# Earlier load requests, and six low parts made by an adding DMA, in an encoder layer

## The chip, the cores and the metric

The kernel runs on one core of a Trainium2 chip. The core has a TensorE for matrix products, a VectorE, a ScalarE and a GpSimd for elementwise work, and a SyncE, which here only issues DMAs. The metric is the device time of one execution in microseconds (us), as the median of several runs. On a page of the profile the engines are PE (matmul), PEld (TensorE's weight loads), DVE (VectorE), ACT (ScalarE), POOL (GpSimd) and SP (SyncE). A q behind such a name is the part of the engine that issues DMAs.

## The reference

One layer over 512 tokens of width 1024, all in fp32. The important lines, with the attention cut:

```python
x = layer_norm(DN_ALPHA * x + 0.5 * swiglu(x, ffn1_wg[i], ffn1_wu[i], ffn1_wd[i]), ln1_g[i], ln1_b[i])
h = x @ w_in[i]
q, k, v, qi, ki, wi, bg, cg, u = jnp.split(h, split_points, axis=-1)
attn = dsa_attention(q, k, v, qi, ki, wi * IDX_SCALE)
conv = short_conv_mixer(bg, cg, u, conv_w[i])
mix = jnp.concatenate([attn, conv], axis=-1) @ w_out[i]
x = layer_norm(DN_ALPHA * x + mix, ln2_g[i], ln2_b[i])
x = layer_norm(DN_ALPHA * x + 0.5 * swiglu(x, ffn2_wg[i], ffn2_wu[i], ffn2_wd[i]), ln3_g[i], ln3_b[i])
x = x + jax.nn.sigmoid(x @ ple_gate_w[i]) * (p[i] @ ple_proj_w[i])
```

with `swiglu(x, wg, wu, wd) = (silu(x @ wg) * (x @ wu)) @ wd` and a hidden width of 2816 (22 chunks of 128).

## The kernel before

**Products.** Every fp32 matrix is held as two tiles of TensorE's faster type fp32r: `hi`, the matrix rounded, and `lo`, what the rounding left. `mm` (L127 to L133) makes each product as three passes, hi·hi, hi·lo and lo·hi. So each weight that comes from memory has to be split before TensorE can read it: `split` (L110 to L112) makes `hi` by a cast on ScalarE and then `lo = src - hi` by a subtraction on VectorE, which therefore waits for the cast.

**Units and pages.** `unit` (L114 to L122) takes a page, loads 512 KB of a weight into it by a DMA that SP issues (L118), takes two more pages for `hi` and `lo`, splits, and gives the first page back. Pages are 38 tiles of one size, handed out and given back first in, first out while the program is built, so a load waits until whoever read its page last is done.

**Order of work.** A scheduler lists all instructions by priority, which is by default the order in which the code is written. `tc.high_priority(offset=n)` moves what is written under it n places earlier. Each engine then works through its own list in order, and so do SP and POOL with the DMAs that they issue. A load and its split stand under the same offset: `AHEAD` and its sisters.

**Stages.** The time falls into the first FFN (to about 320 us) with its norm, the projection by `w_in`, the indexer and the attention, the out-projection with the second norm, the second FFN (from about 629 to 920 us) with its norm, and the gated embedding at the end. In an FFN the first two column chunks are made by `plain` (L256), with one unit of wg and one of wu each; the second FFN alone lets `plain` load the units of its chunk 0 itself, since for the first FFN they are made ahead and handed in. The other 20 chunks go in pairs through `two` (L309), which saves products by sums of weight blocks: for each of wg and wu the generator `weights` (L276) first loads two pages, then splits them and makes and splits the sums S1 to S4, in four steps, and `two` interleaves the steps of wg and wu. So the loads of wu stand behind wg's first step. The rows of wd are units as well (`wd_rows`, L359).

**The second norm's place.** The attention goes head by head: scores, softmax (VectorE L693, ScalarE's exponential L694, VectorE's scale L696), transposes (L710, with casts and subtractions behind them) and the product with the values (L722). Copies of an embedding stage that fills TensorE's gaps (L433) lie in between. Behind it come the four units of w_out, under `AHEAD_O2`, and for each of four token blocks the out-projection (two halves), a sum with x on VectorE and its statistics (L757, L758), the norm `ln_tb` (L156 to L162), and `Quarters.block` (L191), which transposes the block for the second FFN and splits and copies it (L204, L205, L224). In `ln_tb` VectorE adds up the statistics (L158, L159), POOL takes one over the square root by a power (L160), and VectorE scales and shifts the block (L161, L162). POOL does little else here.

Of the kernel before, what the change touches and what calls it, by code (L numbers as in the profile page):

```python
# [10 lines left out]
ALU = mybir.AluOpType  # L11
# [19 lines left out]
WSTEPS = (1, 2, 1)  # L31
BANKS = ((0, 1), (4, 5), (6,), (7, 2, 3))
AHEAD = 25
AHEAD_N = 150
AHEAD2 = 400
AHEAD_D1 = 125
# [9 lines left out]
AHEAD_C = 50  # L46
AHEAD_Q = 50
AHEAD_O = 0
AHEAD_O2 = 75
OB = ("fill", "all", "all", "all")  # L50
AHEAD_G = 200
NWARM = 2
# [11 lines left out]
def layer_kernel(ctx: ExitStack, tc: tile.TileContext, x, ln1_g, ln1_b, ffn1_wg, ffn1_wu, ffn1_wd, w_in,  # L64
# [21 lines left out]
    def page(shape, dt=F32R):  # L86
        i = free_pages.pop(0)
        t = sb.tile(shape, dt, tag=f"pg{i}", name=f"pg{i}_{count('pg')}")
        owner[id(t)] = (i, t)
        return t  # L90
# [19 lines left out]
    def split(hi, lo, src):  # L110
        nc.scalar.copy(hi, src)  # L111
        nc.vector.tensor_sub(lo, src, hi.bitcast(F32))  # L112

    def unit(src, shape, ahead=AHEAD):  # L114

        with tc.high_priority(offset=ahead):
            r = page(shape, F32)
            nc.sync.dma_start(r, src)  # L118
            hi, lo = page(shape), page(shape)
            split(hi, lo, r)  # L120
            free(r)
        return hi, lo  # L122

    def rows(w, r0, n):
        return w[r0:r0 + n * P].rearrange("(c p) n -> p c n", p=P)
# [118 lines left out]
    def ffn(X, wg, wu, wd, ln_g, ln_b, first, load_nat, groups, nplain, ahead, ahead_f, ahead_d):  # L244
# [11 lines left out]
        def plain(fc, ws, cuts, ah):  # L256

            for nm, w in mats:
                if nm not in ws:
                    ws[nm] = unit(rows(w[:, fc * P:(fc + 1) * P], 0, NDC), [P, NDC, P], ah)  # L260
            ps = {nm: bank("all") for nm, _ in mats}
            for n in range(2):
                for k in range(2):
# [12 lines left out]
        def weights(w, fc, ops, pages):  # L276

            r = []
            for c in (0, 4):
                r.append(page([P, 4, 2 * P], F32))  # L280
                nc.sync.dma_start(r[-1], rows(w[:, fc * P:(fc + 2) * P], c * P, 4))
            A11, A21, A12, A22 = (r[k][:, :, m * P:(m + 1) * P] for k in range(2) for m in range(2))
            a11 = page([P, 2, 4, P])
            split(a11[:, 0], a11[:, 1], A11)
# [24 lines left out]
        def two(fc, ah):  # L309

            W, pages = {nm: {} for nm, _ in mats}, []
            steps = [weights(w, fc, W[nm], pages) for nm, w in mats]
            with tc.high_priority(offset=ah):
                for n in WSTEPS:
                    for g in steps:
                        for _ in range(n):
                            next(g)
# [427 lines left out]


    g_t, b_t = bcast(ln2_g[0]), bcast(ln2_b[0])
    wo = [unit(rows(w_out, c * P, 1), [P, 1, 1024], AHEAD_O2) for c in range(4)]
    X = Quarters()
    for t in range(NTB):  # L750
        stats = ring("st", 4, [P, 2, 6])
# [63 lines left out]
```

## Time and profile before

| | |
|---|---|
| median of 3 runs | 1027.09 us (1025.58 to 1027.44) |
| profiled execution, its own time | 1025.29 us |
| its span | 1023.4 us |
| TensorE busy | 1004.4 us, 98% of the span |
| VectorE busy | 823.5 us, 80% |
| ScalarE busy | 442.6 us, 43% |
| GpSimd busy | 27.0 us, 3% |
| read from the chip's memory | 101.49 MB, 101 GB/s over the span |

The span runs from the first to the last record of the execution. The time of the execution has 1.9 us more, before and behind. Busy shares are means over stages that have different limits, so they say which engine is filled, not what an engine waits for at one place. For that there are the chain of waits (the chain of work that ended last, followed back from the last instruction), the table of stretches (busy time of each engine in a part of the span), and the rows of one engine in order of time, each with the idle time ahead of it and what ended that time. TensorE's granted clock is at its full 2.4 GHz throughout.

### The profile page before, as it was taken

Reading aid. Unit: us, or ns where it says so; the run is one execution under the profiler, and the core shown is the slowest. Engines: PE = TensorE matmul, PEld = TensorE weight load, DVE = VectorE, ACT = ScalarE, POOL = GpSimd, SP = SyncE. Lnnn points to the kernel's source line nnn. Section 1 sums busy time; section 2 is a strip of 40 time slices with the busy share of each in tenths; the row PEclk is TensorE's granted clock in tenths of the full one; section 3 lists DMA queues with packets and bytes.
Section 4 is the critical chain, followed back from the end, with each engine's and each line's share of the span. In section 5 each row is a group of like instructions: output and inputs, shape, how many; then the busy total and the mean of one; then the engine's idle time right before and its main releaser. Section 6 shows DMA issues by size and latency. Waiting matters only on the chain.

```text
span 1023.4 us, 15531 instructions
## 1 busy us (share of the span) xinstructions
PE 1004.4 (98%) x6311; PEld 902.3 (88%) x6311; DVE 823.5 (80%) x1289; ACT 442.6 (43%) x627; POOL 27.0 (3%) x35
## 2 busy tenths in 40 slices
PE   9999999999999989999999999999999999999998
PEld 7989999898998868888878788989999898998787
DVE  7997868978698946999679988896868969698952
ACT  7544334433355225432576736443425324246221
POOL 1000000000002100000000011000000000000100
PEclk9999999999999999999999999999999999999999
DMA  9532324323226322423112222431324322236111
GB/s 306 162 109 83 104 83 145 101 80 113 79 100 200 83 61 62 120 67 84 61 42 103 83 71 94 128 120 45 120 84 144 103 79 89 82 124 226 56 38 51
DMA packets 99606, 104.57 MB, mean 102 GB/s; under 512 B 5968, under 2 KB 82000, under 8 KB 99536
## 3 DMA queue, kind: packets, MB, share of 16 engines
q1 hardware_dynamic: 99536, 103.60, 32.0%
q8 instruction: 49, 0.80, 0.3%
q14 instruction: 21, 0.17, 0.1%
HBM read 101.49 MB, written 2.10 MB: 101 GB/s over the span
## 4 chain that ended last, share of the span: by engine, by line
PE 87%; DVE 4%; DMA 4%; ACT 3%; issue 1%; SPq 1%; POOL 0%; POOLq 0%; ACTq 0%; DVEq 0%
PE bk L132 84%; DVE pg L112 2%; ACT pg L111 2%; DMA pg<-in_ffn_wd_dram 1%; PE bk L524 1%; DMA pg<-in_ffn_wu_dram 1%; PE bk L525 1%; PE bk L722 1%; PE bk L146 1%; DMA pg<-in_x_t_dram 1%; DMA pg<-in_ple_proj_w_dram 1%; ACT a L694 0%; SPq L214 0%; DMA pg<-in_ple_gate_w_dram 0%; DVE nat L162 0%
## 5 line engine op out<-in xcount | busy, mean ns | idle before, releaser
L132 PE MATMUL bk<-pg,pg 128*128 128x256 f32 (+1 forms) x2832 | 496.7, 333 | 4.9 <-DVE pg L112 2.1
L132 PEld LDWEIGHTS bk<-pg,pg 128*128 128x128 f32 x2832 | 427.3, 190 | 57.2 <-DVE pg L112 3.9
L111 ACT CAST pg<-pg 128x1024 fp32r<-128x1024 f32 (+1 forms) x270 | 260.0, 976 | 303.3 <-PE bk L132 76.0
L112 DVE TENSOR_TENSOR pg<-pg,pg 128x1024 fp32r<-128x1024 f32 (+1 forms) x270 | 301.1, 1126 | 38.3 <-ACT pg L111 33.0
L132 PE MATMUL bk<-xq,pg 128*128 128x256 f32 x2208 | 274.7, 284 | 2.2 <-DVE mv L158 1.4
L132 PEld LDWEIGHTS bk<-xq,pg 128*128 128x128 f32 x2208 | 269.4, 192 | 5.9 <-ACT pg L433 1.8
L132 PE MATMUL bk<-xT,pg 128*128 128x512 f32 (+2 forms) x600 | 133.0, 381 | 0.2 <-ACT xT L111 0.2
L132 PEld LDWEIGHTS bk<-xT,pg 128*128 128x128 f32 (+1 forms) x600 | 110.1, 186 | 21.2 <-ACT xT L111 0.5
L132 PE MATMUL bk<-pg,xT 128*128 128x512 f32 (+1 forms) x312 | 69.8, 374 | 2.0 <-DVE nat L394 1.7
L132 PEld LDWEIGHTS bk<-pg,xT 128*128 128x128 f32 x312 | 54.9, 188 | 12.2 <-ACT pg L111 2.1
L336 ACT ACTIVATE a<-pg 128x512 f32<-128x512 f32 x40 | 25.2, 630 | 78.0 <-DVE pg L345 70.8
L111 ACT CAST pg<-hf 128x512 fp32r<-128x512 f32 (+1 forms) x56 | 34.6, 618 | 37.6 <-DVE hf L337 19.3
L112 DVE TENSOR_TENSOR pg<-hf,pg 128x512 fp32r<-128x512 f32 (+1 forms) x56 | 38.7, 690 | 4.1 <-ACT pg L111 3.8
L408 DVE SCALAR_TENSOR_TENSOR nat<-bk,nat 128x512 f32<-128x512 f32 x64 | 40.3, 682 | 1.2 <-PE bk L132 1.2
L345 DVE TENSOR_TENSOR pg<-bk,pg 128x512 f32<-128x512 f32 x20 | 13.8, 691 | 29.3 <-PE bk L132 29.0
L337 DVE TENSOR_TENSOR hf<-a,pg 128x512 f32<-128x512 f32 x40 | 27.5, 688 | 11.8 <-ACT a L336 11.7
L160 POOL TENSOR_TENSOR mv<-mv,mhalf 128x1 f32<-128x1 f32 x12 | 17.8, 1479 | 630.4 <-DVE mv L159 630.4
L112 DVE TENSOR_TENSOR pg<-bk,pg 128x512 fp32r<-128x512 f32 (+2 forms) x37 | 22.5, 626 | 12.8 <-ACT pg L111 12.4
L293 DVE TENSOR_TENSOR pg<-pg,pg 128x512 f32<-128x512 f32 x40 | 27.3, 686 | 5.6 <-DMA pg<-in_ffn_wg_dram 5.0
L299 DVE TENSOR_TENSOR pg<-pg 128x512 f32<-128x512 f32 x40 | 27.4, 685 | 2.5 <-PE bk L132 2.5
L294 DVE TENSOR_TENSOR pg<-pg,pg 128x512 f32<-128x512 f32 x40 | 27.4, 684 | 0.0
L300 DVE TENSOR_TENSOR pg<-pg,pg 128x512 f32<-128x512 f32 x40 | 27.0, 685 | 0.1
(100 smaller groups left out, 614.5 us busy)
## 6 DMA issues: line engine op xcount, KB each, us to landing
pg<-in_ffn_wd_dram SPq DMA_DIRECT2D x44, 512.0 KB, 4.0
pg<-in_ffn_wu_dram SPq DMA_DIRECT2D x43, 512.0 KB, 4.8
pg<-in_ffn_wg_dram SPq DMA_DIRECT2D x43, 512.0 KB, 3.9
pg<-in_w_in_dram SPq DMA_DIRECT2D x28, 512.0 KB, 3.6
pg<-in_w_out_dram SPq DMA_DIRECT2D x8, 512.0 KB, 3.9
pg<-in_ple_gate_w_dram SPq DMA_DIRECT2D x8, 512.0 KB, 3.7
pg<-in_x_t_dram SPq DMA_DIRECT2D x8, 256.0 KB, 5.8
nat<-in_x_dram SPq DMA_DIRECT2D x4, 512.0 KB, 9.2
```

The costliest lines, as they stand in the source:

```text
L111: nc.scalar.copy(hi, src)
L112: nc.vector.tensor_sub(lo, src, hi.bitcast(F32))
L132: nc.tensor.matmul(ps, lhsT=st[a], rhs=mv[b], start=first and i == 0 and k == 0, stop=last and i == n - 1 and k == 2)
L160: nc.gpsimd.tensor_tensor(mv[:, 3:4], mv[:, 2:3], mhalf, op=ALU.pow)
L293: nc.vector.tensor_add(S1, A21, A22)
L294: nc.vector.tensor_sub(S2, S1, A11)
L299: nc.vector.tensor_sub(S3, A11, A21)
L300: nc.vector.tensor_sub(S4, A12, S2)
L336: nc.scalar.activation(s_t, e[m][:, :, 0], AF.Silu)
L337: nc.vector.tensor_mul(h3, s_t, e[m][:, :, 1])
L345: nc.vector.tensor_add(e[0][:, 1], prod("S4", "B22"), u4)
L408: nc.vector.scalar_tensor_tensor(dst, acc[t], CY, dst, op0=ALU.mult, op1=ALU.add)
```

## The change

The change has three parts.

**Loads.** In `unit` the load stands under `ahead + LOAD` (60 places earlier) and the split under `ahead` as before. In `two` the loads of both weights are asked for first, under `ah + LOAD`, and the steps of splitting follow: `weights` now yields once behind its loads.

**Low parts.** `unit` can make `lo` in another way (`add`): ScalarE writes `lo = -r`, which rounds `-r`; a DMA that GpSimd issues then adds `r` to `lo` in place, and the sum of `r` and the rounded `-r` is what the rounding left. ScalarE also casts `r` to `hi`. VectorE has no part in it. Six units are made so: the four of w_out and, by `fc == 0`, those of wg and wu of the second FFN's chunk 0.

**The offset of w_out's units**, `AHEAD_O2`, goes from 75 to 150.

```diff
-AHEAD_O2 = 75
+AHEAD_O2 = 150
...
-    def unit(src, shape, ahead=AHEAD):
-
-        with tc.high_priority(offset=ahead):
+    def unit(src, shape, ahead=AHEAD, add=False):
+
+
+        with tc.high_priority(offset=ahead + LOAD):
             r = page(shape, F32)
             nc.sync.dma_start(r, src)
+        with tc.high_priority(offset=ahead):
             hi, lo = page(shape), page(shape)
-            split(hi, lo, r)
+            if add:
+                nc.scalar.mul(lo, r, -1.0)
+                nc.gpsimd.dma_start(lo, r, accum_op=ALU.add)
+                nc.scalar.copy(hi, r)
+            else:
+                split(hi, lo, r)
             free(r)
         return hi, lo
...
             for nm, w in mats:
                 if nm not in ws:
-                    ws[nm] = unit(rows(w[:, fc * P:(fc + 1) * P], 0, NDC), [P, NDC, P], ah)
+                    ws[nm] = unit(rows(w[:, fc * P:(fc + 1) * P], 0, NDC), [P, NDC, P], ah, fc == 0)
...
             for c in (0, 4):
                 r.append(page([P, 4, 2 * P], F32))
                 nc.sync.dma_start(r[-1], rows(w[:, fc * P:(fc + 2) * P], c * P, 4))
+            yield
...
             steps = [weights(w, fc, W[nm], pages) for nm, w in mats]
+            with tc.high_priority(offset=ah + LOAD):
+                for g in steps:
+                    next(g)
             with tc.high_priority(offset=ah):
                 for n in WSTEPS:
                     for g in steps:
...
-    wo = [unit(rows(w_out, c * P, 1), [P, 1, 1024], AHEAD_O2) for c in range(4)]
+    wo = [unit(rows(w_out, c * P, 1), [P, 1, 1024], AHEAD_O2, True) for c in range(4)]
```

What stands in a row on three engines around the second norm follows, before and after. The changed file is 13 lines longer, so the same code has other line numbers after: L113 is the cast of `split` (L111 before), L121 the load of a unit (L118), L169 the power (L160), L707 the exponential (L694), L446 the copy (L433); L125 to L127 are the new negation, adding DMA and cast. In the names, `pg_548`, `pg_551`, `pg_554` and `pg_557` are the loaded units of w_out, with `hi` and `lo` in the two numbers behind each; `pg_568` and `pg_571` are wg and wu of the second FFN's chunk 0, `pg_575` is wg of chunk 1; `a_5572` is the softmax tile of the last head but one, `a_5668` that of the last.

ScalarE at the end of the attention, before: the first cast of a w_out unit stands behind all casts of the last head but one.

```order
L694 ACTIVATE a_5572,ss_5573<-a_5572,ss_5573 128x384
L433 COPY pg_534_5614<-bk_5615 128x512
L694 ACTIVATE a_5572,ss_5573<-a_5572,ss_5573 128x512
L111 CAST pg_527_5565<-hf_5567 64x512
L111 CAST pg_535_5628<-bk_5623 128x512
L111 CAST pg_536_5636<-bk_5631 128x512
L111 CAST pg_537_5642<-bk_5639 128x256
L433 COPY pg_534_5614<-bk_5645 128x512
L111 CAST pg_549_5796<-pg_548_5794 128x1024
```

ScalarE at the same place, after.

```order
L707 ACTIVATE a_5572,ss_5573<-a_5572,ss_5573 128x384
L125 ACTIVATE pg_550_5797<-pg_548_5794 128x1024
L113 CAST pg_527_5565<-hf_5567 64x512
L127 CAST pg_549_5796<-pg_548_5794 128x1024
L707 ACTIVATE a_5572,ss_5573<-a_5572,ss_5573 128x512
L446 COPY pg_534_5614<-bk_5615 128x512
L113 CAST pg_535_5628<-bk_5623 128x512
L113 CAST pg_536_5636<-bk_5631 128x512
L113 CAST pg_537_5642<-bk_5639 128x256
```

The negation and the cast of that unit now stand ahead of the fourth exponential and of the three casts behind it.

POOL around the second norm, before: nothing stands between the power of the first norm and the four of the second.

```order
L160 TENSOR_TENSOR mv_3704<-mv_3704,mhalf 128x1
L160 TENSOR_TENSOR mv_5851<-mv_5851,mhalf 128x1
L160 TENSOR_TENSOR mv_5906<-mv_5906,mhalf 128x1
L160 TENSOR_TENSOR mv_5959<-mv_5959,mhalf 128x1
L160 TENSOR_TENSOR mv_6016<-mv_6016,mhalf 128x1
```

POOL at the same place, after.

```order
L169 TENSOR_TENSOR mv_3704<-mv_3704,mhalf 128x1
L126 DMA pg_550_5797<-pg_548_5794 128x1024
L126 DMA pg_553_5804<-pg_551_5801 128x1024
L126 DMA pg_556_5811<-pg_554_5808 128x1024
L126 DMA pg_559_5818<-pg_557_5815 128x1024
L126 DMA pg_570_6083<-pg_568_6080 128x1024
L126 DMA pg_573_6090<-pg_571_6087 128x1024
L169 TENSOR_TENSOR mv_5855<-mv_5855,mhalf 128x1
```

All six adding DMAs stand ahead of the second norm's first power.

SP from the second load of w_out's units to the first ones of the second FFN, with what each load waits for, before.

```order
L118 DMA pg_557_5812<-in_w_out_dram 128x1024 [waits DMAHW4_49,PE_49]
L153 DMA pg_546_5790<-in_ln_g_dram 128x1024 [waits DMAHW5_49,PE_49]
L118 DMA pg_548_5794<-in_w_out_dram 128x1024 [waits PE_49]
L118 DMA pg_554_5806<-in_w_out_dram 128x1024 [waits DVE_49,PE_49]
L118 DMA pg_575_6193<-in_ffn_wg_dram 128x8x128 [waits DMAHW4_49,DVE_49]
L118 DMA pg_568_6076<-in_ffn_wg_dram 128x8x128 [waits DMAHW1_49,PE_49]
```

SP at the same place, after.

```order
L121 DMA pg_557_5815<-in_w_out_dram 128x1024 [waits DMAHW4_49,PE_49]
L162 DMA pg_546_5790<-in_ln_g_dram 128x1024 [waits DMAHW5_49,PE_49]
L121 DMA pg_548_5794<-in_w_out_dram 128x1024 [waits PE_49]
L121 DMA pg_554_5808<-in_w_out_dram 128x1024 [waits DVE_49,PE_49]
L121 DMA pg_575_6199<-in_ffn_wg_dram 128x8x128 [waits DMAHW4_49,DMASW3_49,Activation_49]
L121 DMA pg_568_6080<-in_ffn_wg_dram 128x8x128 [waits DMAHW1_49,PE_49]
L121 DMA pg_571_6087<-in_ffn_wu_dram 128x8x128 [waits DMAHW2_49,PE_49]
```

The order of the loads is the same. The load of `pg_575`, whose page held a unit of w_out, waited for VectorE's subtraction of that unit; now it waits for the fourth adding DMA (DMASW3) and for ScalarE.

## Rows read from the trace of the kernel before

**Rows 1.** The page's first part: busy us (share of the span) xinstructions.

```profile
PE 1004.4 (98%) x6311; PEld 902.3 (88%) x6311; DVE 823.5 (80%) x1289; ACT 442.6 (43%) x627; POOL 27.0 (3%) x35
```

**Rows 2.** Stretches: length, busy PE, PEld, DVE, ACT, POOL, PEclk, DMA share, GB/s.

```profile
20.00:318.00 298.00, 298.00 (x2142) 282.77 (x2141) 245.60 (x327) 126.08 (x155) 0.91 (x2) 1.00 0.35 113
...
577.00:598.00 21.00, 19.93 (x104) 15.86 (x103) 17.88 (x38) 14.07 (x30) 0.00 (x0) 1.00 0.32 96
598.00:609.00 11.00, 10.49 (x48) 8.37 (x47) 10.36 (x18) 1.64 (x2) 1.46 (x1) 1.00 0.04 10
609.00:629.00 20.00, 17.57 (x113) 15.17 (x112) 17.85 (x25) 10.26 (x18) 4.37 (x3) 1.00 0.09 27
...
629.00:920.00 291.00, 291.00 (x2080) 275.69 (x2079) 237.33 (x314) 122.47 (x152) 0.00 (x0) 1.00 0.33 105
```

**Rows 3.** The chain of waits, 580 to 600 us: start us, us, what.

```profile
585.10 1.14 DVE pg L112
...
594.40 4.80 DMA pg<-in_ffn_wu_dram
```

**Rows 4.** SP's waits, 550 to 600; its rows; DMA issues with us to landing.

```profile
SPq L118 <- DVE pg L112: 17.3, 3, 9.7
...
572.12 8.66 SPq L118 DMA_DIRECT2D pg<-in_w_out_dram  x2
590.18 3.83 SPq L118 DMA_DIRECT2D pg<-in_ffn_wg_dram  x2
...
pg<-in_w_out_dram SPq DMA_DIRECT2D x1, 512.0 KB, 4.4
...
pg<-in_w_out_dram SPq DMA_DIRECT2D x1, 512.0 KB, 3.1
...
pg<-in_ple_proj_w_dram SPq DMA_DIRECT2D x1, 512.0 KB, 5.2
```

**Rows 5.** Groups by form, 577 to 629 us: xcount | busy, mean ns | idle before.

```profile
L112 DVE TENSOR_TENSOR pg<-pg,pg 128x1024 fp32r<-128x1024 f32 x8 | 9.7, 1220 | 1.2 <-ACT pg L111 1.2
L111 ACT CAST pg<-pg 128x1024 fp32r<-128x1024 f32 x6 | 6.3, 1054 | 2.7 <-DMA pg<-in_ffn_wu_dram 1.6 <-DMA pg<-in_ffn_wg_dram 1.1
```

**Rows 6.** VectorE in time: start us, us, what, xcount, [idle before <-releaser].

```profile
585.02 2.35 DVE L112 TENSOR_TENSOR pg<-pg,pg 128x1024 fp32r<-128x1024 f32 x2
...
597.75 0.69 DVE L757 SCALAR_TENSOR_TENSOR nat<-bk,nat 128x512 f32<-128x512 f32 x1 [0.62 <-PE bk L132]
...
600.30 1.23 DVE L112 TENSOR_TENSOR pg<-pg,pg 128x1024 fp32r<-128x1024 f32 x1 [0.46 <-ACT pg L111]
...
605.15 1.28 DVE L161 SCALAR_TENSOR_TENSOR nat<-nat,mv,pg 128x1024 f32<-128x1024 f32 x1
...
606.95 1.27 DVE L162 SCALAR_TENSOR_TENSOR nat<-nat,mv,pg 128x1024 f32<-128x1024 f32 x1
...
616.84 1.23 DVE L112 TENSOR_TENSOR pg<-pg,pg 128x1024 fp32r<-128x1024 f32 x1 [0.59 <-ACT pg L111]
...
629.27 0.69 DVE L205 TENSOR_TENSOR pg<-bk,pg 128x512 fp32r<-128x512 f32 x1 [1.68 <-ACT pg L204]
```

**Rows 7.** ScalarE in time.

```profile
575.90 0.73 ACT L694 ACTIVATE a<-a,ss 128x512 f32<-128x512 f32 x1
...
577.12 1.33 ACT L111 CAST pg<-bk 128x512 fp32r<-128x512 f32 x3
...
583.88 0.57 ACT L111 CAST pg<-bk 128x512 fp32r<-128x512 f32 x1
```

**Rows 8.** TensorE in time.

```profile
577.76 0.50 PE L722 MATMUL bk<-pg,pg 128*128 128x512 f32 x1 [0.19 <-ACT pg L111]
...
586.29 2.35 PE L132 MATMUL bk<-pg,pg 128*128 128x512 f32 x9 [0.82 <-DVE pg L112]
...
619.41 4.07 PE L132 MATMUL bk<-xq,pg 128*128 128x256 f32 x32 [1.43 <-DVE mv L158]
```

**Rows 9.** POOL in time.

```profile
605.38 1.46 POOL L160 TENSOR_TENSOR mv<-mv,mhalf 128x1 f32<-128x1 f32 x1 [240.49 <-DVE mv L159]
```

More of the change, by code (lines that the diff above doesn't have):

```diff
@@ L33 @@
 AHEAD = 25
+LOAD = 60
 AHEAD_N = 150
```

## The prediction

> **What bounds the kernel now.** I read the page's busy times first, then the table of stretches, then the chain of waits, and last the engines' rows in time where that chain leaves TensorE. TensorE is busy 1004.4 us of a span of 1023.4 [rows 1], and in the two FFN bodies it is busy in every microsecond: 298.00 of 298.00 and 291.00 of 291.00 [rows 2]. It never waits there. Nothing that only makes a load or a split earlier inside those bodies can be seen in the time. What is left to win stands at the seams. The seam that this change touches is the one around the second norm, 577 to 629 us: three stretches of 21, 11 and 20 us with 19.93, 10.49 and 17.57 busy, so 4.0 us idle by the records, with VectorE busy 46.1 of these 52 us and ScalarE 26.0 [rows 2]. The chain of waits runs there from the softmax of the last heads (ScalarE and VectorE) over a split on VectorE (585.10) into TensorE (586.29), and later from a load (594.40) over a ScalarE cast, a VectorE subtraction (600.30) and the norm's first sums into TensorE again [rows 3, 6, 8]. So VectorE is what TensorE waits for at this seam, and the six subtractions that go are in it.
>
> **The change, part by part.**
>
> *Loads further ahead.* In the built order SP's rows stand as before apart from neighbours changing places: in most of the 20 pairs the two loads of wu now stand side by side, and at the end one load of wd passes that of the norm's bias. No load moves past work of another kind, since SP's waits are for pages, not for its place in the order: in 550 to 600 us the longest sum of SP's waits is 17.3 us for subtractions to free a page [rows 4]. The cover is that TensorE never waits in the FFN bodies [rows 2]; I cost this part at nothing, ±0.5 us. If the cover failed, each pair would cost what a late cast costs, some tenths.
>
> *Six subtractions off VectorE.* The group has 8 of them in 577 to 629, 1.22 us each [rows 5]; four of the six that go stand before 591 us (two of them at 585.02) and two, of the first FFN units, at 598 to 601.5 (the second at 600.30) [rows 6]. That is 6 x 1.22 = 7.3 us less on VectorE, of which the first four lie mostly beside ScalarE's chain, and the last two, 2.45 us, on the chain itself.
>
> *Six negations on ScalarE.* No row shows one. The nearest is the cast of the same shape, 1.05 us [rows 5], so 6.3 us more on an engine that has 26.0 of 52 us filled; a plain lower bound is the 0.73 us of an exponential of half the columns [rows 7], an upper one the 1.22 of VectorE's subtraction of that tile [rows 5]. The size matters less than the place. The order puts the negation of the third-loaded w_out unit (and its hi cast) ahead of the fourth exponential of the last head but one and of the four casts behind it. Its load is issued at 572.12 and takes 4.4 us [rows 4], so it lands at 576.5, when that exponential (575.90) had already run [rows 7]. So: negation 576.5 to 577.6, the small cast (0.5, an estimate below the 0.57 of a cast of 128 by 512 [rows 7]), the hi cast (1.05), and the exponential starts at 579.1, 3.2 us later; the cast that started at 577.12 starts at 580.3. TensorE's matmul at 577.76, which followed that cast after 0.19 idle [rows 8], waits for it, to 580.9, 3.1 us. Ahead of it the order now puts the last head's eight score matmuls and one of the fill, which stood behind it: some 1.5 us of work. TensorE so comes out 1.5 us late.
>
> *Up to the first norm sum.* The wait at 585 us for the subtraction (0.82 idle at 586.29 [rows 8]) goes. What is late next is ScalarE: with three more negations of 1.05 us its casts of the last head but one's transposes come at 586.7 and 590.0, the first of them not at 583.88 [rows 7] any more, and TensorE waits for them and for the copies that free its fill banks some 1.4 us in pieces. So nothing is won back by 597 us: VectorE's first norm sum starts at 598.65 instead of 597.75 [rows 6], 0.9 late.
>
> *VectorE from there.* Without the two subtractions and the waits ahead of them (0.46 for the second [rows 6]), five sums and statistics of 0.6 us (a sum is 0.69 [rows 6]) bring it to the scale of token block 0 at 602.4, before 605.15 [rows 6]. That is 2.75 us early, 0.6 of it because one statistic now comes later.
>
> *The added wait: six adding DMAs on the POOL queue.* The order puts all six ahead of the second norm's four powers (L160), and POOL takes its queue in order. The last two wait for negations of the first FFN units, those for their loads; and the first FFN load on SP, at 590.18 before [rows 4], now waits until the fourth adding DMA has read its page, with the loads behind it. Call A the time from the end of a negation to the landing. No row shows an adding DMA. Nearest are loads of the same 512 KB on SP's queue, 3.1 us (alone) to 5.2 us (with others) [rows 4]; an add reads two tiles where a load reads one, so I bound A by 3.1 and 2 x 5.2 = 10.4, and take 5, nearest to the loads that shared the engines. Then: fourth negation done 590.15, FFN loads issued from 595.2 on, three together, the last of them landed at about 601.7 (6.5 us: 1.5 MB at the rate of those loads, and their start); negation, cast, negation to 604.2; issue on POOL, 0.8 us (an estimate between nothing and POOL's 1.46 for a power [rows 9]); power 605.1 to 606.5, and the norm's second half (L162) of block 0 starts at 606.6, against 606.95 [rows 6]. Of the 2.75 us only 0.35 is left; VectorE stands behind that instruction, in order.
>
> *To the end of the seam.* After it VectorE has the same work but that statistic (+0.6), and two of its waits shrink by 0.6 each: the 0.59 for a cast at 616.84, since that subtraction now stands later, and part of 1.68 at 629.27 [rows 6]. Sum for the seam: -0.35 + 0.6 - 1.2 = -0.95. TensorE's own work has room for it: the last long wait, 1.43 at 619.41 [rows 8], is for VectorE.
>
> The sum against the profiled execution: 1025.29 - 0.9 = 1024.4 (span 1023.4, 1.9 around it). That execution is 1.8 below the median of the three runs shown, 1027.09; on the scale of the median, 1027.09 - 0.9 = 1026.2, which I forecast.
>
> The Trainium skill ("DMA: Bandwidth & Descriptors", Anatomy of one DMA) gives a DMA that GpSimd issues as 2.0 us plus its bytes at 436 GB/s, by which 512 KB would take an estimated 3.2 us, the first rival's case, with a sum of about -2. No run here shows such a DMA yet. The same skill ("Collectives: The Full Stack", The bandwidth ceiling) says that a reducing DMA is slow by its two source reads, not by the add; by doubling the bytes of the first rule it would be an estimated 4.4 us, near my 5.
>
> **The rivals.**
>
> *The relief lands in full.* If A is 3.1 to 3.5, the loads wait, as now, for TensorE's last reads of their pages (the one in the chain starts at 594.40 [rows 3]) instead of for the add, the power is done at 605.4 and the seam ends some 2 us early; where the late negation also costs TensorE less than 1.5 us (its load landing a microsecond sooner does that), 3 to 3.5. Time 1023.6 to 1025.1, say 1024.3. For it: the DMA engines are near empty there (a share of 0.04 in 598 to 609 [rows 2]) and the data never leaves the chip's own memory. Against: the negation's place on ScalarE doesn't hang on A.
>
> *The adds are late.* With A = 10.4 the second adding DMA (negation done 584.0) lands at 594.4, where TensorE wants its tile at 588.1: 6 us of TensorE's wait; and the power hangs on the fourth, so that L162 of block 0 starts at 606.6 + 5.4 = 612.0 instead of 606.95. By that the seam ends 4.5 us late: 1027.09 + 4.5 = 1031.6. It turns slower than before from A of about 6 on, and slower by 0.2% from about 8. For it: six of TensorE's matmuls and, over the powers, four of VectorE's instructions now hang on a queue that nothing in this trace has used. Against: slacks of 8, 4, 5 and 7.5 us from the four negations to the first matmul that reads the tile, by the order and the times above.
>
> *The swapped loads open a wait in an FFN body or at the end.* One pair too late costs 0.3 to 1 us, and the last seam, where a wd load and the norm's bias change places, can move by 0.5 either way. Time within 0.2% by itself.
>
> **How the numbers follow.** About 0.2%, 2.05 us, is what a measurement of this kernel can tell from no change. Forecast, A of 4 to 7, with the third rival in it: 0.42, and 0.38 of that within 0.2%, 0.02 to each side. Relief in full: 0.30, and 0.28 of that faster by over 0.2% where the ends are good ones, 0.02 within. Late adds: 0.28, of which 0.25 slower and 0.03 within. So faster 0.30, same 0.43, slower 0.27. The range reaches from 1027.09 - 4.3 (full relief and half a microsecond at the last seam) to 1027.09 + 4.2 (A of about 10): 1022.8 to 1031.3. Signs are mixed in it; the forecast's own range is 1024.8 to 1028.6.
>
> **What would show it.** Right: in the profile after, the exponential ahead of the late cast starts near 579 us, TensorE's wait at 586 for VectorE is gone and shorter waits for ScalarE stand between 578 and 592; landings of the adding DMAs 4 to 6 us after their negations; the first power of the second norm behind the sixth adding DMA, with VectorE idle ahead of L162; FFN bodies without a wait. Wrong: a landing after 3 us or 8 us; a negation far from 1.05 us; a POOL issue of several microseconds, which would hold the power; or TensorE idle in an FFN body.

## The result, and the profile after

The changed kernel takes 1031.91 us (median of 6 runs, 1029.20 to 1034.36), the kernel before beside it 1026.36 us (6 runs): a ratio of 1.0054, interval 1.0036 to 1.0071. It is slower by 5.5 us, where 1026.2 was forecast and 1031.3 was the end of the range. The profiled execution took 1029.20 us, the shortest of the six, against 1025.29: a span of 1027.4 us, 4.0 longer.

The page's first line for the changed kernel: VectorE has 6 us less and ScalarE 6.5 us more than in [rows 1], as was meant.

```profile
PE 1005.4 (98%) x6311; PEld 901.9 (88%) x6311; DVE 817.5 (80%) x1283; ACT 449.1 (44%) x633; POOL 30.7 (3%) x41
```

The same stretches as in [rows 2] (length, busy PE, PEld, DVE, ACT, POOL, PEclk, DMA share, GB/s), with the second FFN's body cut ahead of the wait near 918.

```profile
577.00:598.00 21.00, 17.92 (x92) 13.63 (x91) 13.02 (x33) 17.71 (x35) 3.69 (x4) 1.00 0.62 129
598.00:609.00 11.00, 9.95 (x46) 7.77 (x45) 8.43 (x15) 4.51 (x5) 2.33 (x3) 1.00 0.90 209
609.00:629.00 20.00, 20.00 (x124) 17.54 (x123) 18.69 (x28) 10.03 (x17) 4.37 (x3) 1.00 0.16 40
...
629.00:917.00 288.00, 287.69 (x2050) 272.19 (x2049) 232.77 (x307) 121.07 (x149) 0.00 (x0) 1.00 0.33 105
917.00:960.00 43.00, 40.15 (x257) 35.39 (x256) 37.23 (x48) 19.72 (x25) 1.46 (x1) 1.00 0.45 147
```

In 577 to 598 TensorE idles 3.1 us where it idled 1.1; in 609 to 629 it idles nothing where it idled 2.4. The seam's relief came, and was paid for ahead of it. And 2.9 us idle stand in 917 to 960. The first wait there, 1.43 us up to 918.74, stands ahead of a matmul that ran at 916.17 in the kernel before, inside the body of 629 to 920 that was thought safe; the second stands behind that body. TensorE's rows in time name the waits (start us, us, what, [idle before <-releaser]).

```profile
578.98 0.44 PE L537 MATMUL bk<-pg,pg 128*128 128x384 f32 x1 [0.96 <-DVE ss L706]
...
587.07 0.73 PE L141 MATMUL bk<-pg,pg 128*128 128x512 f32 x2 [0.41 <-ACT pg L446]
589.65 0.50 PE L141 MATMUL bk<-pg,pg 128*128 128x512 f32 x1 [1.13 <-DMA pg<-pg]
...
608.40 1.09 PE L210 MATMUL bk<-ident,nat 128*128 128x128 f32 x8 [1.05 <-DVE nat L171]
...
661.58 1.46 PE L141 MATMUL bk<-xq,pg 128*128 128x256 f32 x10 [0.31 <-DVE pg L114]
...
918.74 5.90 PE L141 MATMUL bk<-xq,pg 128*128 128x256 f32 x47 [1.43 <-ACT pg L113]
945.93 12.81 PE L141 MATMUL bk<-pg,pg 128*128 128x512 f32 x53 [1.08 <-ACT pg L113]
```

**Where the 4.0 us went.** TensorE runs 6311 matmuls in every kernel here, so I compared the start of the n-th one in two traces, for n of 3360, 3726, 4124, 5618, 5825, 6035 and 6138 (in the kernel before at 560, 632, 690, 900, 925, 962 and 985 us). The growth of the difference from one to the next is what a stretch lost against the first profile of the kernel before; the changed kernel comes to the first of them 0.31 early, and loses the last 0.12 at its end.

| profile | 560–632 | 632–690 | 690–900 | 900–925 | 925–962 | 962–985 |
|---|---|---|---|---|---|---|
| changed kernel | +0.73 | +0.57 | 0.00 | +1.54 | +1.30 | +0.05 |
| before, taken again (e5) | −0.03 | 0.00 | 0.00 | +0.09 | +0.69 | +1.39 |
| loads alone (e1) | +1.54 | 0.00 | 0.00 | +0.71 | +1.24 | +1.53 |
| adds and offset (e2) | +1.90 | 0.00 | 0.00 | +0.04 | +0.71 | +0.33 |
| e2 and single loads (e3) | +2.04 | 0.00 | 0.00 | +0.03 | +1.72 | +1.57 |
| e2 and pair loads (e4) | +0.51 | +0.07 | 0.00 | +1.66 | +0.86 | +1.32 |
| adds, chunk 0 alone (e6) | −2.52 | +0.63 | 0.00 | +0.08 | −0.04 | +0.01 |
| adds, w_out alone (e7) | +5.53 | 0.00 | 0.00 | +0.08 | −0.21 | +3.18 |
| changed, last pair back (e8) | +5.06 | 0.00 | 0.00 | +0.04 | +1.27 | −0.02 |
| changed, offset 75 (e9) | +3.26 | 0.00 | 0.00 | +0.56 | +1.57 | −0.03 |
| before, offset 150 (e10) | +3.52 | 0.00 | 0.00 | +0.25 | +1.11 | +3.04 |
| e2, pages held (e11) | +5.09 | 0.00 | 0.00 | 0.00 | +0.21 | −0.11 |
| adds, chunks 0 and 1 (e12) | −3.39 | 0.00 | 0.00 | +0.08 | +0.58 | +1.34 |

The unchanged kernel alone moves by 1.39 in the last column and 0.69 in the one before it, so single profiles settle nothing there. Every number of 1.3 and more in the last column comes with a wait of TensorE of 1.8 to 2.0 us for the third norm, which e5 has too; in e7 and e10 the granted clock fell behind it. The columns 560–632 and 900–925 are quiet in the unchanged kernel (0.03 and 0.09), but in e1 and in e7 to e11 the number in 560–632 holds a fall of the clock besides the waits (see the last section). The +0.57 in 632–690 stands in two kernels that have no part of the change in common but the adds of chunk 0, and not in others that have them.

### The profile page after: what moved, and what is told of

It reads as the page before. It is cut to its first block, busy times and chain, and to the rows that moved or that the text cites. A ratio compares the mean times of both kernels' runs of the same rounds, so it can differ in the third digit from the quotient of the medians.

```text
span 1027.4 us, 15552 instructions
## 1 busy us (share of the span) xinstructions
PE 1005.4 (98%) x6311; PEld 901.9 (88%) x6311; DVE 817.5 (80%) x1283; ACT 449.1 (44%) x633; POOL 30.7 (3%) x41
## 4 chain that ended last, share of the span: by engine, by line
PE 82%; DMA 5%; DVE 5%; issue 3%; ACT 3%; SPq 1%; POOL 1%; POOLq 0%; ACTq 0%; DVEq 0%
PE bk L141 79%; DVE pg L114 2%; ACT pg L113 2%; DMA pg<-in_ffn_wd_dram 1%; PE bk L537 1%; DMA pg<-in_w_in_dram 1%; PE bk L538 1%; DMA pg<-in_ffn_wu_dram 1%; DMA pg<-in_x_t_dram 1%; DMA pg<-in_ple_proj_w_dram 1%; DMA pg<-pg 1%; PE bk L735 1%; DVE nat L171 1%; POOL mv L169 0%; PE bk L155 0%
## 5 line engine op out<-in xcount | busy, mean ns | idle before, releaser
L113 ACT CAST pg<-pg 128x1024 fp32r<-128x1024 f32 (+1 forms) x264 | 253.5, 974 | 295.0 <-PE bk L141 63.4
L114 DVE TENSOR_TENSOR pg<-pg,pg 128x1024 fp32r<-128x1024 f32 (+1 forms) x264 | 294.0, 1124 | 48.8 <-ACT pg L113 42.0
L113 ACT CAST pg<-hf 128x512 fp32r<-128x512 f32 (+1 forms) x56 | 34.6, 619 | 38.3 <-DVE hf L350 20.4
L169 POOL TENSOR_TENSOR mv<-mv,mhalf 128x1 f32<-128x1 f32 x12 | 17.2, 1432 | 393.6 <-DVE mv L168 393.6
```

The source lines that it names most:

```text
L169: nc.gpsimd.tensor_tensor(mv[:, 3:4], mv[:, 2:3], mhalf, op=ALU.pow)
```

## The experiments

Ratios are to the kernel before on the same chip; its medians there were 1027.66 (e1 to e4), 1027.48 (e5 to e8) and 1027.60 us (e9 to e12). Ratios and intervals are the record's estimates and not quotients of the medians, so e3 can have the larger median and e4 the larger ratio.

| kernel | median, us | ratio | interval |
|---|---|---|---|
| e1 loads alone | 1030.44 | 1.0028 | 1.0016 to 1.0040 |
| e2 adds and offset | 1029.73 | 1.0023 | 1.0008 to 1.0038 |
| e3 e2 and single loads | 1032.39 | 1.0039 | 1.0022 to 1.0055 |
| e4 e2 and pair loads | 1031.96 | 1.0046 | 1.0028 to 1.0064 |
| e6 adds, chunk 0 alone | 1026.22 | 0.9984 | 0.9975 to 0.9994 |
| e7 adds, w_out alone, offset 150 | 1034.52 | 1.0068 | 1.0055 to 1.0080 |
| e8 changed, last pair back | 1030.77 | 1.0031 | 1.0017 to 1.0046 |
| e9 changed, offset 75 | 1032.72 | 1.0052 | 1.0038 to 1.0066 |
| e10 before, offset 150 | 1029.75 | 1.0027 | 1.0016 to 1.0039 |
| e11 e2, pages held | 1032.06 | 1.0042 | 1.0026 to 1.0057 |
| e12 adds, chunks 0 and 1 | 1024.44 | 0.9973 | 0.9962 to 0.9984 |

### The two halves of the change (e1, e2)

e1 leaves the adds and the offset out of the changed kernel, e2 the earlier loads.

```diff
-AHEAD_O2 = 150
+AHEAD_O2 = 75
...
-            if add:
-                nc.scalar.mul(lo, r, -1.0)
-                nc.gpsimd.dma_start(lo, r, accum_op=ALU.add)
-                nc.scalar.copy(hi, r)
-            else:
-                split(hi, lo, r)
+            split(hi, lo, r)
```

> Loads asked for earlier alone: no adding DMA, AHEAD_O2 at 75. Theory L (the loss of the changed kernel lies in the second FFN's last pair, where TensorE stands 1.43 us ahead of 918.74 for a cast that the new order puts late, and in the third norm's place behind it): 2 to 3.5 us above the kernel before, 1028.4 to 1029.9 against 1026.4, with that wait of 1.4 us again near 916 to 919 and a wait of about 1 us for a load of wd near 945. Theory A (the adding DMAs cost it all): within 0.5 us of the kernel before. On the clock: if its falls (0.996 and 0.997 in four of six runs of the changed kernel) come with the loads, some runs here show them; if with the adds, all runs show 0.999 or 1.000.

```diff
-LOAD = 60
+LOAD = 0
...
-            yield
...
-            with tc.high_priority(offset=ah + LOAD):
-                for g in steps:
-                    next(g)
```

> Six adding DMAs and AHEAD_O2 at 150 alone, all loads asked for as before. Theory L: 0 to 1 us above the kernel before, 1026.4 to 1027.4, the FFN bodies without a wait, and the seam with the waits of the changed kernel (0.96 near 579, 1.13 for the second adding DMA near 589.7, 1.05 near 608.4). Theory A: 3 to 5.5 us above, 1029.4 to 1031.9. On the clock: if the adds bring its falls, several runs show 0.996 to 0.998 and lie 2 to 4 us above the fastest; if not, all show 0.999 or 1.000 and lie within 2 us of each other.

Neither theory holds alone: each half costs about 2.5 us, 0.28% and 0.23%, together 0.51% against the change's 0.54%. In e1 the wait near 918 is there (0.58), and the seam lost too, though it has no add in it. Its TensorE row there, and the stretch behind it, where the clock fell:

```profile
621.17 5.56 PE L136 MATMUL bk<-xq,pg 128*128 128x256 f32 x32 [2.76 <-DVE mv L162]
...
621.00:625.00 4.00, 3.83 (x19) 3.86 (x20) 4.00 (x8) 0.00 (x0) 1.46 (x1) 0.57 0.02 4
```

The wait of 1.43 of [rows 8] has become 2.76. ScalarE shows what changed ahead of it: the cast of chunk 1's wu (L113), which stood behind a block's two casts, now stands ahead of them (L208) and waits for its load. That this alone makes the wait longer is not shown; no run moves this cast by itself.

```profile
616.33 1.05 ACT L113 CAST pg<-pg 128x1024 fp32r<-128x1024 f32 x1 [0.39 <-DMA pg<-in_ffn_wu_dram]
617.28 1.07 ACT L208 CAST xq<-bk 128x512 fp32r<-128x512 f32 x2
```

So an earlier load does not leave the split where it was. The changed kernel does not have this wait of 2.76, so e1's 0.28% is not wholly what the loads cost in it; the step from e2 to the changed kernel, 0.23% to 0.54%, says 0.31%. In e2 the FFN body is clean and the seam has the changed kernel's waits, somewhat longer (1.35, 1.24, 1.75).

### The single loads and the pairs' loads (e3, e4)

e3 is the changed kernel with `two` as before (the last two parts of e2's diff), e4 the changed kernel with `ahead + LOAD` in `unit` back at `ahead`.

> The changed kernel, but the two weights of a pair load as before (each weight's loads with its first step of splitting); single units still load 60 places earlier, and the six adds stay. If the loss in the last pair comes from the pairs' loads: the wait of 1.4 us near 918 goes, and the time is about that of the adds alone plus what the single units' earlier loads (the order of two loads near the third norm) cost, 0 to 1 us. If it comes from the single units' loads: the wait near 918 stays, and the time is that of the changed kernel.

> The changed kernel, but with single units loading as before (load and split under one offset); the pairs' loads stay first, 0 places earlier than their splits, and the six adds stay. If the pairs' loads standing first (not the 60 places) are what moves the splits of the last pair: the wait near 918 is there again, some 1.4 us, and the time is 1 to 3 us above that of the adds alone. If the 60 places are: no wait there, the time of the adds alone.

By the ratios the single loads add 0.16% to e2 and the pairs' loads 0.23%, each with an interval that overlaps e2's; where they stand is read from the profiles. The pairs' loads make the wait at 918: e4 has it, e3 does not. In the column 900–925 the four profiles with all pairs' loads first lost 0.56 to 1.66, eight without them at most 0.25. (The expectation of e4 speaks of 0 places for the pairs' loads; its edit leaves their 60 places, so standing first and the 60 places are not told apart.)

```profile
919.19 5.90 PE L141 MATMUL bk<-xq,pg 128*128 128x256 f32 x47 [1.53 <-ACT pg L113]
```

The single loads cost in 925–962: with them 1.24 to 1.72 in five profiles, without them −0.21 to 1.11 in eight, 0.5 in the mean. That is about 0.9 us, from ranges that nearly touch. In the changed kernel's chain of waits it is a load of wd (issued 939.06, 5.75 us) and the cast behind it, for which TensorE waits 1.08:

```profile
939.06 5.75 DMA pg<-in_ffn_wd_dram
...
944.83 1.05 ACT pg L113
...
945.93 0.51 PE bk L141
```

### The last pair undone (e8)

```diff
-            with tc.high_priority(offset=ah + LOAD):
-                for g in steps:
-                    next(g)
+            back = fc == 20 and load_nat is None
+            if not back:
+                with tc.high_priority(offset=ah + LOAD):
+                    for g in steps:
+                        next(g)
             with tc.high_priority(offset=ah):
-                for n in WSTEPS:
+                for i, n in enumerate(WSTEPS):
                     for g in steps:
-                        for _ in range(n):
+                        for _ in range(n + (back and i == 0)):
                             next(g)
```

> The changed kernel, but the last pair of the second FFN loads and splits as before (each weight's loads with its first step). Theory L: TensorE's wait of 1.4 to 1.5 us near 918 goes, all else stays, and the time is 1 to 2 us below the changed kernel's, 0.35 to 0.45% above the kernel before. Rival (the two loads of wu beside wg's are late by themselves): a wait of the same size comes back elsewhere between 900 and 945.

The wait near 918 goes (0.04 in the column) and none comes in its place; 1.0031 against 1.0054, though the intervals overlap: somewhat more than theory L expected. (Its seam is the changed kernel's, instruction for instruction; that this profile lost 5.06 us there is taken up below.) What the change did there stands in ScalarE's order. Before, from the cast of the last wd unit on:

```
L111 CAST pg_861_8879<-hf_8875 128x512
L111 CAST pg_895_9143<-pg_893_9139 128x512
L111 CAST pg_899_9153<-pg_894_9141 128x1024
L336 ACTIVATE a_9067<-pg_884_8932 128x512
...
```

and after:

```
L113 CAST pg_861_8885<-hf_8881 128x512
L113 CAST pg_899_9159<-pg_894_9147 128x1024
L349 ACTIVATE a_9073<-pg_884_8938 128x512
L113 CAST pg_888_9076<-hf_9072 128x512
L113 CAST pg_909_9179<-pg_907_9175 128x1024
L113 CAST pg_903_9167<-pg_901_9163 128x1024
L113 CAST pg_897_9153<-pg_893_9145 128x512
```

The cast of wg's first block (`pg_893`), which the pair's first products read, stood second and now stands seventh, behind the casts of two sums. In time, on ScalarE after:

```profile
909.39 1.05 ACT L113 CAST pg<-pg 128x1024 fp32r<-128x1024 f32 x1 [2.66 <-DMA pg<-in_ffn_wg_dram]
914.26 0.63 ACT L349 ACTIVATE a<-pg 128x512 f32<-128x512 f32 x1 [3.82 <-DVE pg L358]
...
916.18 3.98 ACT L113 CAST pg<-pg 128x1024 fp32r<-128x1024 f32 x5
```

That cast, third of the five, runs at 918.08, and TensorE goes on at 918.74; in the kernel before it ran at 905.72. Its place held it and not its load, which had landed at 907.86, ten us earlier. The two loads of wg do take longer, 6.7 us with a load of wu beside them and 5.5 before:

```profile
pg<-in_ffn_wg_dram SPq DMA_DIRECT2D x2, 512.0 KB, 6.7
...
pg<-in_ffn_wg_dram SPq DMA_DIRECT2D x2, 512.0 KB, 5.5
```

### The kernel before again, and the adds taken apart (e5, e6, e7)

> The kernel before, unchanged, profiled beside the next three on one chip, since execution lists show clocks of 0.997 and 0.998 for it too. Expected: 1025 to 1029 us; the seam of 577 to 629 with the waits of the first trace (0.8, 0.5, 0.8, 1.4); if the clock is below 1.000, its fall stands near 361 to 365, where it stands in all four experiments so far and where the changed kernel's own profile has none.

The one run of the kernel before took 1027.63 us. Its seam is that of the first profile. Against the expectation its clock did not fall near 361; which profiles have that fall is told in the last section.

e6 has adding DMAs for chunk 0 alone, with all loads as before and AHEAD_O2 at 75; e7 for w_out alone, at 150. Against e2:

```diff
-AHEAD_O2 = 150
+AHEAD_O2 = 75
...
-    wo = [unit(rows(w_out, c * P, 1), [P, 1, 1024], AHEAD_O2, True) for c in range(4)]
+    wo = [unit(rows(w_out, c * P, 1), [P, 1, 1024], AHEAD_O2) for c in range(4)]
```

> Adding DMAs for wg and wu of the second FFN's chunk 0 alone; w_out's units split as before, AHEAD_O2 at 75, all loads as before. Theory S (the seam loses because the first FFN load waits for the fourth adding DMA, and the norm's power for that load's negation on POOL's queue): without the four adds of w_out the loads start as before (590 to 594.4), the first power starts near 603 instead of 605.4, and TensorE gains 1 to 2 us in the seam: 0 to 2 us below the kernel before. Rival P (an adding DMA ahead of the power on POOL's queue costs by itself, some 1.9 us for two issues of 0.87): 0 to 2 us above.

```diff
-                    ws[nm] = unit(rows(w[:, fc * P:(fc + 1) * P], 0, NDC), [P, NDC, P], ah, fc == 0)
+                    ws[nm] = unit(rows(w[:, fc * P:(fc + 1) * P], 0, NDC), [P, NDC, P], ah)
```

> Adding DMAs for the four units of w_out alone, AHEAD_O2 at 150; the FFN units split as before, all loads as before. Theory S: the first FFN load still waits for the fourth adding DMA (some 6 us later than in the kernel before), its cast and subtraction stand in VectorE's way as before, and TensorE still waits for the second adding DMA (about 1.2): 1.5 to 4 us above the kernel before. Rival P: without adds between the loads and the power, POOL is free: within 1 us of the kernel before.

This is the clearest pair: the two adds of chunk 0 gain 0.16%, the four of w_out with their offset cost 0.68%. POOL's rows of e6 and e7 show the norm's first power at 603.04 and at 610.36, against 605.38 before [rows 9].

```profile
600.20 1.05 POOL L126 DMA_DIRECT2D pg<-pg  x1 [235.79 <-PE bk L141]
602.08 0.87 POOL L126 DMA_DIRECT2D pg<-pg  x1 [0.83 <-DVE nat L766]
603.04 1.47 POOL L169 TENSOR_TENSOR mv<-mv,mhalf 128x1 f32<-128x1 f32 x1
...
610.36 1.46 POOL L169 TENSOR_TENSOR mv<-mv,mhalf 128x1 f32<-128x1 f32 x1 [16.31 <-DVE mv L168]
```

Two issues ahead of the power cost nothing in e6, since POOL was idle: rival P falls. TensorE idles nothing in the middle of e6's seam, where it idled 0.5 [rows 2]:

```profile
598.00:609.00 11.00, 11.00 (x55) 9.05 (x54) 10.40 (x20) 5.59 (x8) 3.39 (x3) 1.00 0.69 142
```

In e7 POOL is idle for 16.31 us and the power is late all the same, for the FFN loads start at 597.77 (590.53 in e5), and their casts and subtractions stand ahead of the norm. So theory S has the direction of e7 and not its size: 0.68% is some 7 us, and it expected 1.5 to 4. TensorE's waits there, and the stretch behind the second, in which the clock fell:

```profile
590.96 0.50 PE L141 MATMUL bk<-pg,pg 128*128 128x512 f32 x1 [1.02 <-DMA pg<-pg]
...
613.24 1.29 PE L210 MATMUL bk<-ident,nat 128*128 128x128 f32 x8 [2.30 <-DVE nat L171]
...
614.00:618.00 4.00, 4.00 (x14) 3.24 (x12) 4.00 (x8) 2.28 (x4) 1.45 (x1) 0.57 0.00 0
```

### The offset (e9, e10)

e9 is the changed kernel and e10 the kernel before, each with the other's AHEAD_O2.

> The changed kernel with AHEAD_O2 back at 75, so that w_out's negations stand behind the casts of the last head but one on ScalarE. Theory O (the place of the negations and casts on ScalarE costs TensorE its waits of 0.96 near 579 and 0.4 near 587): those waits go, and the time is 1 to 2 us below the changed kernel's, 0.2 to 0.4% above the kernel before. Rival Q (a negation that comes later makes its adding DMA land later, and the fourth one is what the first FFN load waits for): TensorE's wait for an adding DMA grows from 1.1 to 3 us or more, the power comes later too, and the time is 1 to 4 us above the changed kernel's.

> The kernel before with AHEAD_O2 at 150 alone: no adding DMA, all loads as before; w_out's casts stand earlier on ScalarE, one of them ahead of the fourth exponential of the last head but one. Theory O: that cast waits for its load (landing near 576.5) and TensorE waits near 579 for the exponential's users, 0.5 to 1.5 us; the wait of 0.8 at 586 goes; the sum 0 to 1.5 us above the kernel before. Rival: the two cancel, or the earlier splits help: within 0.5 us or below.

The offset costs 0.27% by itself, more than theory O's 1.5 us. (The kept profile is of the longest of e10's twelve runs, 1034.43 us, so its seam's 3.52 is not typical.) ScalarE in e10: a cast of w_out waits 1.33 us for its load, ahead of an exponential that was ready, and TensorE waits 1.62 behind both.

```profile
578.36 1.05 ACT L111 CAST pg<-pg 128x1024 fp32r<-128x1024 f32 x1 [1.33 <-DMA pg<-in_w_out_dram]
...
579.83 0.72 ACT L694 ACTIVATE a<-a,ss 128x512 f32<-128x512 f32 x1
...
581.31 0.74 PE L132 MATMUL bk<-pg,pg 128*128 128x512 f32 x2 [1.62 <-DVE pg L112]
```

Taking the offset from the changed kernel helps nothing (1.0052 against 1.0054): the early waits go, and TensorE waits for two adding DMAs instead, as rival Q had it, with a fall of the clock between the two. Neither O's gain nor Q's loss of 1 to 4 us came.

```profile
587.61 0.96 PE L141 MATMUL bk<-pg,pg 128*128 128x512 f32 x3 [1.85 <-DMA pg<-pg]
590.08 2.93 PE L141 MATMUL bk<-pg,pg 128*128 128x512 f32 x6 [1.51 <-DMA pg<-pg]
...
588.00:596.00 8.00, 6.49 (x22) 5.04 (x20) 1.62 (x3) 3.21 (x6) 0.00 (x0) 0.57 0.47 94
```

The offset was there to give the adds time. At neither of the two offsets that were run do w_out's adds pay: at 150 they hold ScalarE, at 75 TensorE.

### Pages held (e11)

Against e2, the pages of w_out's loaded units are given back only behind the norm:

```diff
+                if held is not None:
+                    held.append(r)
+                    return hi, lo
...
-    free(g_t, b_t, *attnT)
+    free(g_t, b_t, *attnT, *raw)
```

> Six adds and AHEAD_O2 at 150 with all loads as before, as in the run of the adds alone, but the pages of w_out's loaded units are given back only behind the norm, so that the first FFN loads take other pages and wait for TensorE alone, not for the fourth adding DMA. Theory S: those loads start near 595 instead of 598.5, the first power ends some 3 us earlier, and the time is 1 to 3 us below that of the adds alone, 0 to 1 us above the kernel before; TensorE's wait of about 1.2 for the second adding DMA stays. Rival: the loads wait for TensorE's last reads until 597 anyway, and the gain is under 0.5 us.

The first FFN loads start at 595.80 and the first power at 603.90, as expected, and the kernel is no faster (1.0042 against e2's 1.0023). With the pages in another order chunk 1's loads come at 614 to 616 us, and their casts stand on ScalarE, each behind a wait for its load, ahead of the third block's. TensorE's row, and the stretch with it:

```profile
625.96 5.49 PE L144 MATMUL bk<-pg,pg 128*128 128x512 f32 x12 [2.94 <-ACT pg L236]
...
625.00:632.00 7.00, 6.04 (x16) 4.88 (x17) 4.77 (x7) 2.32 (x5) 1.45 (x1) 0.51 0.14 27
```

The expectation looked at one wait and not at who takes the pages next.

### Adds for chunks 0 and 1 (e12)

Against e6, `fc == 0` becomes `fc < 2 and load_nat is None` (the second FFN alone).

> Adding DMAs for wg and wu of the second FFN's chunks 0 and 1, none for w_out; all else as the kernel before. Two more subtractions of 1.22 us leave VectorE between 611 and 621, where it is 17.9 of 20 us busy, and two more issues stand on POOL between the second and the third power. Theory S: the negations of chunk 1 have their loads by 595 and 615, POOL is free there, and TensorE's wait of 1.46 near 620 shrinks: 0.5 to 1.5 us below the kernel with chunk 0 alone, 0.2 to 0.35% below the kernel before. Rival: the load of chunk 1's wu (issued near 611, landed near 615) holds the third power on POOL's queue, and the time is 0 to 3 us above that with chunk 0 alone.

It is faster than both kernels: 0.27% below the kernel before, as theory S expected. (e6's interval overlaps its own, so the step from e6 is less sure.) Of TensorE's waits in the second half of the seam (1.43 us alone for one in [rows 8]) one of 0.61 is left.

```profile
619.25 1.06 PE L210 MATMUL bk<-ident,nat 128*128 128x128 f32 x8 [0.61 <-DVE nat L171]
```

## Why the prediction was wrong, point by point

**What bounds the kernel.** Right for the seam: less work for VectorE there is worth 2.5 us (e6) and 3.4 us (e12) in the profiles' column 560–632, and 0.16 and 0.27% in the times. Wrong in the use made of "TensorE never waits in the bodies". It shows that earlier splits win nothing; it does not show that later ones cost nothing, and the change made some later.

**Loads further ahead, costed at 0 ± 0.5.** This is the step that failed, with the seam's sum below as the second. It read SP's rows and took the splits to stay where they were. Nothing was hidden: the built order of the changed kernel, which was read for SP, has on ScalarE the cast of `pg_893` five rows later. Measured: +2.9 us for the half alone (e1, 1.6 to 4.1); in the changed kernel's profile +1.54 in the last pair and +1.30 around the third norm, of which e3 and e4 against the rest leave some 0.9 to the single loads. The third rival had the mechanism, a pair too late for 0.3 to 1 us, and put it within 0.2%.

**Six negations on ScalarE.** The places and sizes were right: one negation 1.06 us, the exponential at 578.85 where 579.1 was written.

```profile
576.43 1.06 ACT L125 ACTIVATE pg<-pg 128x1024 fp32r<-128x1024 f32 x1 [1.06 <-DMA pg<-in_w_out_dram]
...
578.85 0.72 ACT L707 ACTIVATE a<-a,ss 128x512 f32<-128x512 f32 x1
```

TensorE came to 598 some 2.0 us late by its idle time (3.1 against 1.1), where 1.5 were written. VectorE's first norm sum came at 600.12 (598.65 written) and block 0's scale at 603.89 (602.4): 1.5 us late, but the power, which waits for the adds, came later still.

**The second adding DMA.** The sum had A = 5 and a slack of 4 us from the second negation to the matmul that reads its tile, and yet no wait for it: a slip in the working. Measured from the six negations' ends to the landings, A was 5.1, 5.8, 4.8, 4.9, 4.9 and 5.7 us, and TensorE waited 1.13 at 589.65, more than the 0.82 for VectorE that went. With a load or another add beside it A reached 7.5 (e8) and 8.6 us (e9). The page's row for the adding DMAs, from issue to landing:

```profile
pg<-pg POOLq DMA_DIRECT2D x6, 512.0 KB, 4.7
```

Of the two estimates drawn from the Trainium skill, that from "DMA: Bandwidth & Descriptors" (Anatomy of one DMA), 3.2 us, is too short here, and that which counts the source twice after "Collectives: The Full Stack" (The bandwidth ceiling), 4.4, is near the 4.7 measured.

**The wait on SP and POOL.** Right in mechanism and nearly in size. The fourth adding DMA is issued at 591.84 and landed at 596.42; the first FFN load starts at 596.47 (595.2 written), its adds are issued from 603.68, the power runs to 607.03 (606.5) and the norm's second half starts at 607.06 (606.6).

```profile
591.84 0.90 POOL L126 DMA_DIRECT2D pg<-pg  x1 [2.08 <-ACT pg L125]
603.68 0.88 POOL L126 DMA_DIRECT2D pg<-pg  x1 [10.95 <-PE bk L141]
...
606.15 0.88 POOL L169 TENSOR_TENSOR mv<-mv,mhalf 128x1 f32<-128x1 f32 x1
...
596.47 1.11 SPq L121 DMA_DIRECT2D pg<-in_ffn_wg_dram  x2
...
607.06 1.28 DVE L171 SCALAR_TENSOR_TENSOR nat<-nat,mv,pg 128x1024 f32<-128x1024 f32 x1 [1.30 <-POOL mv L169]
```

**The seam's sum.** −0.95 was forecast; +0.73 came in the profile, and +0.23% (about 2.4 us) for adds and offset alone (e2). The sum followed VectorE and said that TensorE's own work had room for it. That failed: by its idle time TensorE was 2.0 us later at 598, with the second adding DMA's wait in it, and 0.5 more at 609, behind the norm's second half; from 609 to 629 it then worked without a pause, so its own work set the end. The 2.4 us of idle time that it had there were all its room. 0.3 of the +0.73 came ahead of 577, and some 0.3 I have not traced. But the profile is that of the shortest run. Four profiles that have this seam (changed kernel, e2, e3, e4) lost 0.5 to 2.0, and e8, with the changed kernel's own seam, 5.06. There the clock fell at 583. Counted from the seam's start, the second negation ended 0.9 us later and a load of w_out was issued 1.8 us later, so that the adding DMA went out ahead of that load (586.66 and 587.07) and not behind it (584.15 and 583.62), and landed 7.5 us after the negation and not 5.8. TensorE waited, and the clock fell again:

```profile
583.00:587.00 4.00, 4.00 (x15) 3.39 (x15) 2.71 (x9) 2.85 (x8) 0.34 (x1) 0.57 0.23 42
...
593.88 0.79 PE L141 MATMUL bk<-pg,pg 128*128 128x512 f32 x1 [2.16 <-DMA pg<-pg]
```

That is the rival of late adds, in one execution, with A at 7.5 for one add beside a load. Whether it is why the six runs of the changed kernel spread over 5.2 us, with mean clocks from 0.996 to 1.000, is not shown: beside e9 to e12 the kernel before, which has no add, spread over 4.3 us with the same clocks, and where the clock fell in the five runs that left no trace was not recorded.

**Relief in full.** The relief was there, 2.4 us of idle time in 609 to 629. It belongs to the adds of chunk 0 (e6, e12) and was given back by w_out's adds and their offset (e7, e10). The prediction treated the six as one thing with one A; they were two with opposite signs.

**The range.** It ended at 1031.3 with late adds as the only cause. About half of the slowdown came from a step that had ±0.5 in it.

What stays open: why the scheduler moved the cast of `pg_893` when only loads were moved; how much of 925 to 962 belongs to the single loads (0.9 us between ranges that nearly touch), and the places of the clock's falls in runs without a trace.

## What to carry to other kernels

A load asked for earlier does not come alone: in the order that this scheduler built, casts behind it changed places on ScalarE, so the order of every engine that uses the data has to be compared, not the load queue's alone. "The busy engine never waits here" covers work that comes earlier and not work that comes later. An adding DMA of 512 KB took 4.8 to 6.1 us from its source's readiness to its landing in most cases, and up to 8.6 beside other transfers. It paid for chunks 0 and 1 (0.27% faster), whose tiles TensorE first reads 16 to 22 us after the negation, and not for w_out, where they are wanted 4.7 to 8.3 us after it and a load waits for the page that the fourth one reads.

## What the runs showed of the hardware

TensorE's granted clock fell from 2.4 to 1.2 GHz near 361 us in 8 of 14 profiles, of changed and unchanged loads and adds alike (0.57 to 0.66 of full speed over the 4 us from 361), and each of these lost 0.9 to 1.3 us from 355 to 400. Up to 575 us the engines' orders of e2, e3, e6, e7, e10, e11 and e12 are that of the kernel before; the first five have the fall, the last two and both profiles of the kernel before have not, so the order does not decide it. In all 14 TensorE had waited 1.7 to 2.1 us just before for the first norm, as long in those without a fall. The same stretch of e2, which has it, and of the kernel before, which has not:

```profile
361.00:365.00 4.00, 4.00 (x13) 3.10 (x12) 3.63 (x6) 0.93 (x1) 1.42 (x1) 0.57 0.49 131
...
361.00:365.00 4.00, 4.00 (x20) 3.30 (x19) 3.29 (x6) 0.73 (x1) 1.52 (x1) 1.00 0.47 131
```

The busy time is the same 4.00 us, and 13 matmuls start where 20 did. In the seam falls begin within a wait of TensorE or up to 1.1 us behind it, in e1 (2.76 us), e7 (2.30), e8 (2.16), e9 (1.85), e10 (2.80) and e11 (2.94), while e3 had a wait of 2.28 without one; e8's first fall, at 583, stands 2.3 us behind a wait of 1.04. So a wait there can cost more than its length, and not in every execution.

An adding DMA occupied POOL for 0.87 to 1.06 us at its issue.
